# SwiGLU of a two-layer decoder trunk: three products of 256 columns per k tile in place of one of 512 and one of 256

## The chip, the cores and the metric

The kernel runs on one core of one Trainium2 chip. The metric is the device time of one execution in microseconds (us). Engines are named as the profile names them: PE is TensorE (PEld its weight loads), DVE is VectorE, ACT is ScalarE, POOL is GpSimd, SP is the engine that issues the transfers.

## The reference

Two layers over 256 tokens of width 1024, all float32. Each layer normalises x, projects it (6 parts of attention and recurrence, two gates), runs two token mixers, merges them through two projections, and adds the result to x. Then comes the part that is changed, a SwiGLU with 2816 hidden columns:

```python
h = rms_norm(x, norm_ffn[l])
x = x + (jax.nn.silu(h @ w_gate[l]) * (h @ w_up[l])) @ w_down[l]
```

## The kernel before

Everything is held transposed: 128 features on the partitions, 256 tokens (`T`) along the row. `xT` holds x in `KD` = 8 tiles of 128 features; the hidden width is `KF` = 22 such tiles.

**Products in float32 from two halves.** TensorE runs on a rounded float32 (`F32R`). So that nothing is lost, each operand a is split into a rounded part ah and the rest al, and a·b becomes ah·bh + ah·bl + al·bh. For the data, `split` (L207 to L214) does it: ScalarE writes the rounded part, VectorE the rest. For the weights, `load` (L102 to L123) fetches a chunk of about 1 MB by one transfer on SP's queue into `stage` (3 buffers), and for each half of the chunk (1024 columns, eight weight tiles) ScalarE casts it to `wh` (L118) and VectorE subtracts to get `wl` (L120). `wh` and `wl` have five buffers each. `weights` asks for a chunk and for the next one (L125 to L128).

**Two forms of the sum.** `mm3` (L216 to L229) makes the three products one by one, each of 256 columns into one result of 256 columns: L227 (ah·bh), L228 (ah·bl), L229 (al·bh). The input projections, the merge projections (L825) and the output projection (L842) use it. `mmw` (L231 to L236) is used by the SwiGLU alone. There the data tile holds bh and bl side by side (512 columns), and

```python
PE.matmul(ps, ah, b, start=i == 0, stop=False)
PE.matmul(ps[:, 0], al, b[:, 0], start=False, stop=i == n - 1)
```

makes ah·[bh bl] in one product of 512 columns (L235), then al·bh in one of 256 (L236). The result is a whole PSUM bank whose two halves have still to be added. Every product loads its own weight tile first (a LDWEIGHTS with the line of its product).

**The SwiGLU** (L849 to L886). `norm_in` (L283 to L290) splits xT times the norm's gain into `xx` and works out 1/rms per token on the way: sums of squares (L244, L246, L250), token sums on TensorE (L257, four products), a power on GpSimd (L201), and a product with ones (L275) that spreads the result over the partitions, copied to `rb` (L280). The products of the SwiGLU begin ahead of that; rb scales their results.
- Gate and up: for each m of 22, two results (j = 0 gate, j = 1 up), each over 8 k tiles. For each j: `mmw` into a bank of its own, ScalarE copies the second half out (L862), VectorE adds the first half (L863), and VectorE (j = 0) or GpSimd (j = 1) multiplies by rb (L864). Then tanh (L866), the silu (L867), the product with up on GpSimd (L869), and a split into `ff2` (L870).
- Down: for each m of 8, `mmw` over 22 k tiles into a bank, and VectorE adds both halves to xT, one after the other (L883). In the last layer each m is sent out (L885).

Eight PSUM banks are shared by four pools of two: `acc`, `prj`, `trp`, `hgp`. Even m use acc and trp, odd m hgp and prj.

**What sets the order.** Each engine works through its own queue in order. The order of the instructions in the queues is made by the scheduler of the tile framework from a simulated timeline; only the opening of layer 0 has an order written by hand (L322). Several products without their last tiles of xx can thus be begun ahead of the norm.

Of the kernel before, what the change touches and what calls it, by code (L numbers as in the profile page):

```python
# [9 lines left out]
F32 = mybir.dt.float32  # L10
# [5 lines left out]
ALU = mybir.AluOpType  # L16
AX = mybir.AxisListType

P = 128
T = 256  # L20
TT = T // P
D = 1024
KD = D // P
# [59 lines left out]
def trunk(ctx: ExitStack, tc: tile.TileContext, x_in, w_in, vec_in, gqk_in, cst_in, msk_in, out):  # L83
    nc = tc.nc
    V, S, G, PE = nc.vector, nc.scalar, nc.gpsimd, nc.tensor
# [6 lines left out]
    acc = ctx.enter_context(tc.tile_pool(name="acc", bufs=2, space=bass.MemoryType.PSUM))  # L92
    prj = ctx.enter_context(tc.tile_pool(name="prj", bufs=2, space=bass.MemoryType.PSUM))
    trp = ctx.enter_context(tc.tile_pool(name="trp", bufs=2, space=bass.MemoryType.PSUM))
    hgp = ctx.enter_context(tc.tile_pool(name="hgp", bufs=2, space=bass.MemoryType.PSUM))
# [29 lines left out]
    def weights(l, n, between=None):  # L125
        i = order.index((l, n, dict(PLAN)[n]))
        load(i + 2, between)
        return ready.pop((l, n))  # L128
# [10 lines left out]
    xT = cp.tile([P, KD, T], F32, name="xT")  # L139
# [63 lines left out]
    def bc(ap, shape):  # L203
        return ap.broadcast_to(shape)


    def split(hi, lo, src, scale=None):  # L207

        if scale is None:
            S.copy(hi, src)  # L210
            V.tensor_tensor(lo, src, hi.bitcast(F32), ALU.subtract)
        else:
            S.activation(hi, src, AF.Copy if isinstance(scale, float) else AF.Identity, scale=scale)  # L213
            V.scalar_tensor_tensor(lo, src, scale, hi.bitcast(F32), ALU.mult, ALU.subtract)  # L214

    def mm3(ps, pairs, late=False, opens=True, closes=True):  # L216
        n = len(pairs)
        if late:
            for i, ((ah, al), (bh, bl)) in enumerate(pairs):
                PE.matmul(ps, ah, bh, start=i == 0, stop=False)  # L220
                PE.matmul(ps, ah, bl, start=False, stop=False)
            for i, ((ah, al), (bh, bl)) in enumerate(pairs):
                PE.matmul(ps, al, bh, start=False, stop=i == n - 1)
            return
        shared = not (opens and closes)
        for i, ((ah, al), (bh, bl)) in enumerate(pairs):
            PE.matmul(ps, ah, bh, start=opens and i == 0, stop=False, skip_group_check=shared)  # L227
            PE.matmul(ps, ah, bl, start=False, stop=False, skip_group_check=shared)  # L228
            PE.matmul(ps, al, bh, start=False, stop=closes and i == n - 1, skip_group_check=shared)  # L229

    def mmw(ps, items):  # L231

        n = len(items)
        for i, ((ah, al), b) in enumerate(items):
            PE.matmul(ps, ah, b, start=i == 0, stop=False)  # L235
            PE.matmul(ps[:, 0], al, b[:, 0], start=False, stop=i == n - 1)  # L236

    def squares(src, kt, both=False):

# [20 lines left out]
    def token_stats(src, kt, both=False):  # L260
        return token_sums(squares(src, kt, both))

    def norm_rows(ss, meanwhile=None):

        ms = wk.tile([P, TT], F32, name="ms")
        V.tensor_scalar(ms, ss, 1.0 / D, EPS, ALU.mult, ALU.add)
        r = lay.tile([P, TT], F32, name="r")
        ins = power(r, ms)
        dg = wk.tile([P, TT, P], F32, tag="gs", name="dg")
        for t in range(TT):  # L270
            V.tensor_scalar(dg[:, t], ident, r[:, t:t + 1], None, ALU.mult)
        if meanwhile:
            meanwhile()
        ps = prj.tile([P, 512], F32, name="prj")
        PE.matmul(ps[:, :T], ones, dg.rearrange("p t c -> p (t c)"), start=True, stop=True)  # L275
        return r, ins, ps

    def norm_cols(ps):
        rb = lay.tile([P, T], F32, name="rb")
        S.copy(rb, ps[:, :T])  # L280
        return rb

    def norm_in(l, col):  # L283

        xx = lay.tile([P, KD, 2, T], F32R, name="xx")
        xh, xl = xx[:, :, 0], xx[:, :, 1]
        for k in range(KD):
            split(xh[:, k], xl[:, k], xT[:, k], vec[:, l, col + k:col + k + 1])
        r, _, ps = norm_rows(token_stats(xT, KD, both=True))
        return xx, xh, xl, r, norm_cols(ps)  # L290
# [25 lines left out]
    for l in range(L):  # L316
        opening = ExitStack()
        if l:
            xx, xh, xl, r, rb = norm_in(l, V_MIX)
        else:  # L320

            opening.enter_context(tc.manual_schedule())  # L322
            xx, ps0 = first()
            xh, xl = xx[:, :, 0], xx[:, :, 1]
# [33 lines left out]
            rb = norm_cols(said[2])  # L358
# [4 lines left out]
        xs = [(xh[:, k], xl[:, k]) for k in range(KD)]  # L363
# [173 lines left out]
        W = weights(l, "ukv")  # L537
# [4 lines left out]
        for i in range(2):  # L542
            W = weights(l, f"uq{i}")
# [18 lines left out]
        ah = mixp.tile([P, 4, T], F32R, tag="B", name="ah")  # L562
        al = mixp.tile([P, 4, T], F32R, tag="C", name="al")
# [255 lines left out]
        for i in range(2):  # L819
            Ws = [weights(l, f"proj{2 * i + c}") for c in range(2)]  # L820
            pss = [(acc.tile([P, 2, T], F32, name="acc") if c < 2 else prj.tile([P, 2, T], F32, name="prj")) for c in range(4)]
            for s, (sh, sl) in enumerate(((ah, al), (bh, bl))):
                for c in range(4):
                    o = (c % 2 * 2 + s) * 4 * P
                    mm3(pss[c][:, s], [(Ws[c // 2](o + k * P, P), (sh[:, k], sl[:, k])) for k in range(4)])  # L825
            for c in range(4):
                m = 4 * i + c
                g = wk.tile([P, 2, T], F32, name="gs", bufs=2)
# [5 lines left out]
        for i in range(4):  # L834
            W = weights(l, f"out{i}")
            ps = acc.tile([P, 2, T], F32, name="acc")

            step = KD if i else KD // 2
            for k0 in range(0, KD, step):
                for j in range(2):  # L840
                    o = j * KD * P
# [5 lines left out]


        xx, xh, xl, r, rb = norm_in(l, V_FFN)  # L849
        ffp = tc.alloc_tile_pool(name=f"ffn{l}", bufs=1)  # L850
        ff2 = ffp.tile([P, KF, 2, T], F32R, name="ff2")
        for m in range(KF):
            W = weights(l, f"gu{m}")
            if m % 2 == 0:
                pss = [acc.tile([P, 2, T], F32, name="acc"), trp.tile([P, 2, T], F32, name="trp")]
            else:
                pss = [hgp.tile([P, 2, T], F32, name="hgp"), prj.tile([P, 2, T], F32, name="prj")]
            g = ffp.tile([P, 2, T], F32, name="g", bufs=2)
            for j, ps in enumerate(pss):
                o = j * KD * P  # L860
                mmw(ps, [(W(o + k * P, P), xx[:, k]) for k in range(KD)])
                S.copy(g[:, j], ps[:, 1])  # L862
                V.tensor_tensor(g[:, j], g[:, j], ps[:, 0], ALU.add)  # L863
                (V, G)[j].tensor_tensor(g[:, j], g[:, j], rb, ALU.mult)  # L864
            th = ffp.tile([P, T], F32, name="th", bufs=2)
            S.activation(th, g[:, 0], AF.Tanh, scale=0.5)  # L866
            V.scalar_tensor_tensor(th, th, 1.0, g[:, 0], ALU.add, ALU.mult)  # L867
            hd = ffp.tile([P, T], F32, name="hd", bufs=2)
            G.tensor_tensor(hd, th, g[:, 1], ALU.mult)  # L869
            split(ff2[:, m, 0], ff2[:, m, 1], hd, 0.5)  # L870

        cur = None
        for m in range(KD):
            ps = acc.tile([P, 2, T], F32, name="acc")
            items = []
            for k in range(KF):
                i = m * KF + k
                if cur is None or cur[0] != i // 16:
                    cur = (i // 16, weights(l, f"dn{i // 16}"))
                items.append((cur[1]((i % 16) * P, P), ff2[:, k]))  # L880
            mmw(ps, items)
            for j in range(2):
                V.tensor_tensor(xT[:, m], xT[:, m], ps[:, j], ALU.add)  # L883
            if l == L - 1:
                nc.sync.dma_start(out[:, m], xT[:, m])  # L885
        ffp.release()  # L886
# [84 lines left out]
```

## Time and profile before

| | |
|---|---|
| time, median of 3 runs | 767.38 us (767.37 to 767.92) |
| profiled execution, its own time | 767.33 us |
| its span, first to last instruction | 765.5 us |
| PE busy | 758.3 us (99%), 5676 products |
| PEld busy | 693.4 us (91%), 5676 loads |
| DVE busy | 584.9 us (76%) |
| ACT busy | 443.7 us (58%) |
| POOL busy | 259.5 us (34%) |
| granted TensorE clock, mean | 0.999 |
| read from HBM | 131.11 MB, 173 GB/s over the span |

PE is a product, PEld a weight load, which overlaps products. Products are pipelined: the profile models their ends, and several are in flight at a time, so a busy PE only says that there is always one under way. How fast they follow each other is seen in the starts, in the timeline. A line such as `acc<-xx,wh` says that the tile acc is written from xx and wh; buffer numbers are left out.

### The profile page before, as it was taken

The numbers are of one execution on the slowest core, as the hardware profiler recorded it, in microseconds if no ns is written. First come the engines' busy times: TensorE is split into PE (matmuls) and PEld (weight loads), VectorE is DVE, ScalarE is ACT, GpSimd is POOL, SyncE is SP. The second block draws the span as 40 slices with busy tenths as digits, with TensorE's granted clock in tenths as the row PEclk, the third lists the DMA queues.
The fourth block names the chain that finished last, engine by engine and source line by source line (L and its number), as shares of the span: only waits on it lengthen the run. The fifth ranks groups of instructions, "written<-read, shape, count | busy, mean of one in ns | idle before, by whom it ended". The sixth has DMA issues, their size and how long they took to land.

```text
span 765.5 us, 14316 instructions
## 1 busy us (share of the span) xinstructions
PE 758.3 (99%) x5676; PEld 693.4 (91%) x5676; DVE 584.9 (76%) x866; ACT 443.7 (58%) x811; POOL 259.5 (34%) x275
## 2 busy tenths in 40 slices
PE   9999999999999999999999999999999999999998
PEld 6899999999988888888899999999998888888886
DVE  6799876678898888866667988757888988887542
ACT  6668766545465556554447796654565655655330
POOL 0685422024333443411126823201432444443000
PEclk9999999999999999999999999999999999999999
DMA  7654434436565555555534544444465555646630
GB/s 280 221 175 166 166 116 161 166 116 212 168 220 176 209 170 202 180 185 199 196 118 166 181 154 167 134 143 165 167 221 168 188 195 174 211 166 200 206 124 21
DMA packets 20802, 133.07 MB, mean 174 GB/s; under 512 B 2432, under 2 KB 3712, under 8 KB 5504
## 3 DMA queue, kind: packets, MB, share of 16 engines
q1 hardware_dynamic: 20736, 132.17, 51.0%
q8 instruction: 44, 0.72, 0.4%
q14 instruction: 22, 0.18, 0.1%
HBM read 131.11 MB, written 1.05 MB: 173 GB/s over the span
## 4 chain that ended last, share of the span: by engine, by line
PE 93%; issue 2%; POOL 1%; DVE 1%; DMA 1%; ACT 1%; SPq 1%; POOLq 0%
PE acc L235 16%; PE acc L227 11%; PE acc L229 11%; PE acc L228 10%; PE acc L236 8%; PE hgp L235 5%; PE prj L235 5%; PE trp L235 5%; PE prj L236 3%; PE trp L236 3%; PE hgp L236 3%; PE prj L227 2%; PE prj L229 2%; PE prj L228 2%; PE prj L570 1%
## 5 line engine op out<-in xcount | busy, mean ns | idle before, releaser
L120 DVE TENSOR_TENSOR wl<-st,wh 128x1024 fp32r<-128x1024 f32 (+3 forms) x241 | 322.0, 1337 | 74.1 <-ACT wh L118 72.8
L118 ACT CAST wh<-st 128x1024 fp32r<-128x1024 f32 (+3 forms) x249 | 257.1, 1038 | 139.2 <-PE acc L235 64.3
L227 PE MATMUL acc<-xx,wh 128*128 128x256 f32 x472 | 133.5, 283 | 0.0
L229 PE MATMUL acc<-xx,wl 128*128 128x256 f32 x472 | 132.3, 281 | 0.3 <-DVE wl L120 0.3
L228 PE MATMUL acc<-xx,wh 128*128 128x256 f32 x472 | 132.2, 280 | 0.0
L235 PE MATMUL acc<-ff,wh 128*128 128x512 f32 x352 | 124.3, 397 | 0.0
L236 PE MATMUL acc<-ff,wl 128*128 128x256 f32 x352 | 98.6, 281 | 0.0
L229 PEld LDWEIGHTS acc<-xx,wl 128*128 128x128 f32 x472 | 88.9, 189 | 1.4 <-issue 0.9
L227 PEld LDWEIGHTS acc<-xx,wh 128*128 128x128 f32 x472 | 89.0, 188 | 0.8 <-issue 0.2
L228 PEld LDWEIGHTS acc<-xx,wh 128*128 128x128 f32 x472 | 88.9, 188 | 0.7 <-issue 0.7
L864 POOL TENSOR_TENSOR g<-g,rb 128x256 f32<-128x256 f32 x44 | 37.2, 846 | 135.5 <-DVE g L863 123.1
L235 PEld LDWEIGHTS acc<-ff,wh 128*128 128x128 f32 x352 | 66.0, 188 | 16.2
L869 POOL TENSOR_TENSOR hd<-th,g 128x256 f32<-128x256 f32 x44 | 66.1, 1504 | 7.4 <-DVE th L867 4.5
L213 ACT ACTIVATE ff<-hd 128x256 fp32r<-128x256 f32 x44 | 18.4, 419 | 84.6 <-POOL hd L869 84.6
L236 PEld LDWEIGHTS acc<-ff,wl 128*128 128x128 f32 x352 | 66.1, 188 | 0.2
L235 PE MATMUL prj<-xx,wh 128*128 128x512 f32 x176 | 63.5, 399 | 0.0
L235 PE MATMUL acc<-xx,wh 128*128 128x512 f32 x176 | 63.3, 397 | 0.0
L235 PE MATMUL hgp<-xx,wh 128*128 128x512 f32 x176 | 63.2, 397 | 0.0
L235 PE MATMUL trp<-xx,wh 128*128 128x512 f32 x176 | 63.1, 397 | 0.0
L250 POOL TENSOR_TENSOR sq<-sq 128x256 f32<-128x256 f32 x27 | 26.3, 974 | 88.5 <-ACT sq L244 53.9
L236 PE MATMUL acc<-xx,wl 128*128 128x256 f32 x176 | 49.6, 282 | 0.0
L236 PE MATMUL hgp<-xx,wl 128*128 128x256 f32 x176 | 49.5, 281 | 0.0
(259 smaller groups left out, 1732.1 us busy)
## 6 DMA issues: line engine op xcount, KB each, us to landing
st<-in_w_dram SPq DMA_DIRECT2D x115, 1024.0 KB, 4.8
st<-in_w_dram SPq DMA_DIRECT2D x4, 1088.0 KB, 5.0
st<-in_w_dram SPq DMA_DIRECT2D x4, 576.0 KB, 3.8
st<-in_w_dram SPq DMA_DIRECT2D x3, 512.0 KB, 6.8
xT<-in_x_dram SPq DMA_DIRECT2D x4, 256.0 KB, 5.5
out_dram<-xT SPq DMA_DIRECT2D x8, 128.0 KB, 1.9
st<-in_w_dram SPq DMA_DIRECT2D x2, 256.0 KB, 4.1
cst<-in_cst_dram SPq DMA_DIRECT2D x1, 260.0 KB, 7.6
```

What stands on the lines that cost most here:

```text
L118: S.copy(wh[:, :n_], st[:, c:c + n_])
L120: eng.tensor_tensor(wl[:, :n_], st[:, c:c + n_], wh[:, :n_].bitcast(F32), ALU.subtract)
L213: S.activation(hi, src, AF.Copy if isinstance(scale, float) else AF.Identity, scale=scale)
L227: PE.matmul(ps, ah, bh, start=opens and i == 0, stop=False, skip_group_check=shared)
L228: PE.matmul(ps, ah, bl, start=False, stop=False, skip_group_check=shared)
L229: PE.matmul(ps, al, bh, start=False, stop=closes and i == n - 1, skip_group_check=shared)
L235: PE.matmul(ps, ah, b, start=i == 0, stop=False)
L236: PE.matmul(ps[:, 0], al, b[:, 0], start=False, stop=i == n - 1)
L250: G.tensor_tensor(tot, tot, sq, ALU.add)
L570: PE.matmul(pv[:, h], qT[:, h0 + h, t * P:(t + 1) * P], kT[:, h0 + h, :ns], start=True, stop=True)
L864: (V, G)[j].tensor_tensor(g[:, j], g[:, j], rb, ALU.mult)
L869: G.tensor_tensor(hd, th, g[:, 1], ALU.mult)
```

## The change

Gate and up, and down, go through `mm3` as the other projections do; `mmw` goes. The gate and the up result of one m share one bank (256 columns each), from `acc` for even and `prj` for odd m, and are scaled by rb straight from the bank by one instruction of VectorE. The copy on ScalarE, the addition on VectorE, and the scaling on GpSimd go. In down, one addition to xT takes the place of two. Weight chunks, their conversions, transfers and buffers stay.

```diff
-    def mmw(ps, items):
-
-        n = len(items)
-        for i, ((ah, al), b) in enumerate(items):
-            PE.matmul(ps, ah, b, start=i == 0, stop=False)
-            PE.matmul(ps[:, 0], al, b[:, 0], start=False, stop=i == n - 1)
...
         xx, xh, xl, r, rb = norm_in(l, V_FFN)
+        xs = [(xh[:, k], xl[:, k]) for k in range(KD)]
         ffp = tc.alloc_tile_pool(name=f"ffn{l}", bufs=1)
         ff2 = ffp.tile([P, KF, 2, T], F32R, name="ff2")
         for m in range(KF):
             W = weights(l, f"gu{m}")
-            if m % 2 == 0:
-                pss = [acc.tile([P, 2, T], F32, name="acc"), trp.tile([P, 2, T], F32, name="trp")]
-            else:
-                pss = [hgp.tile([P, 2, T], F32, name="hgp"), prj.tile([P, 2, T], F32, name="prj")]
+            ps = (acc, prj)[m % 2].tile([P, 2, T], F32, name=("acc", "prj")[m % 2])
+            for j in range(2):
+                o = j * KD * P
+                mm3(ps[:, j], [(W(o + k * P, P), xs[k]) for k in range(KD)])
             g = ffp.tile([P, 2, T], F32, name="g", bufs=2)
-            for j, ps in enumerate(pss):
-                o = j * KD * P
-                mmw(ps, [(W(o + k * P, P), xx[:, k]) for k in range(KD)])
-                S.copy(g[:, j], ps[:, 1])
-                V.tensor_tensor(g[:, j], g[:, j], ps[:, 0], ALU.add)
-                (V, G)[j].tensor_tensor(g[:, j], g[:, j], rb, ALU.mult)
+            V.tensor_tensor(g, ps, bc(rb.unsqueeze(1), [P, 2, T]), ALU.mult)
             th = ffp.tile([P, T], F32, name="th", bufs=2)
...
-                items.append((cur[1]((i % 16) * P, P), ff2[:, k]))
-            mmw(ps, items)
-            for j in range(2):
-                V.tensor_tensor(xT[:, m], xT[:, m], ps[:, j], ALU.add)
+                items.append((cur[1]((i % 16) * P, P), (ff2[:, k, 0], ff2[:, k, 1])))
+            mm3(ps[:, 0], items)
+            V.tensor_tensor(xT[:, m], xT[:, m], ps[:, 0], ALU.add)
```

## Rows read from the trace of the kernel before

**Rows 1.** The page: the span, and the chain that ended last by engine
```profile
span 765.5 us, 14316 instructions
...
PE 93%; issue 2%; POOL 1%; DVE 1%; DMA 1%; ACT 1%; SPq 1%; POOLq 0%
```

**Rows 2.** Busy time by engine and count, then granted clock (PEclk), in three stretches
```profile
core 0: us, PE busy (x) PEld busy (x) DVE busy (x) ACT busy (x) POOL busy (x), PEclk, DMA share, GB/s
220.00:320.00 100.00, 100.00 (x568) 86.89 (x567) 85.14 (x128) 57.92 (x109) 44.28 (x38) 1.00 0.56 188
...
160.00:200.00 40.00, 40.00 (x355) 40.00 (x354) 33.45 (x43) 22.28 (x33) 15.10 (x13) 1.00 0.55 186
443.00:448.00 5.00, 5.00 (x45) 5.00 (x44) 5.00 (x9) 4.87 (x14) 0.75 (x2) 1.00 0.24 43
```

**Rows 3.** Timeline of TensorE: first pair of layer 0's down projection, and what follows the 176 pairs
```profile
325.33 0.40 PE L235 MATMUL acc<-ff,wh 128*128 128x512 f32 x1
...
387.50 0.28 PE L227 MATMUL acc<-xx,wh 128*128 128x256 f32 x1
```

**Rows 4.** Timeline of TensorE, input projection of layer 1, a stretch without a break
```profile
442.75 0.28 PE L227 MATMUL acc<-xx,wh 128*128 128x256 f32 x1
...
447.81 0.28 PE L228 MATMUL acc<-xx,wh 128*128 128x256 f32 x1
```

**Rows 5.** Timeline of TensorE: first product of L842 in layer 0, and what follows the 192
```profile
178.33 0.28 PE L227 MATMUL acc<-yh,wh 128*128 128x256 f32 x1
...
200.12 0.39 PE L235 MATMUL acc<-xx,wh 128*128 128x512 f32 x1
```

**Rows 6.** Timeline of TensorE, a later input projection of layer 1, without a break
```profile
517.54 0.28 PE L227 MATMUL acc<-xx,wh 128*128 128x256 f32 x1
...
522.99 0.28 PE L227 MATMUL acc<-xx,wh 128*128 128x256 f32 x1
```

**Rows 7.** Timeline of TensorE around the ones product of layer 1's first norm
```profile
398.44 0.59 PE L275 MATMUL prj<-dg,cst 128*128 128x256 f32 x2
...
398.99 0.28 PE L227 MATMUL hgp<-xx,wh 128*128 128x256 f32 x1
399.11 0.28 PE L228 MATMUL hgp<-xx,wh 128*128 128x256 f32 x1
...
399.90 0.28 PE L229 MATMUL hgp<-xx,wl 128*128 128x256 f32 x1
```

**Rows 8.** Timeline of TensorE around the token sums of that norm
```profile
393.51 0.50 PE L257 MATMUL trp<-cst,sq 128*128 128x1 f32 x4
...
394.08 0.28 PE L229 MATMUL acc<-xx,wl 128*128 128x256 f32 x1
...
394.55 0.28 PE L227 MATMUL acc<-xx,wh 128*128 128x256 f32 x1
```

**Rows 9.** Timeline of TensorE just after the token sums ahead of layer 0's SwiGLU
```profile
207.26 0.39 PE L235 MATMUL acc<-xx,wh 128*128 128x512 f32 x1
...
207.60 0.39 PE L235 MATMUL trp<-xx,wh 128*128 128x512 f32 x1
...
207.95 0.40 PE L235 MATMUL trp<-xx,wh 128*128 128x512 f32 x1
```

**Rows 10.** The groups by line: a 512-element product with rb, DVE's addition, ACT's copy
```profile
L395 DVE TENSOR_TENSOR gs<-acc,rb 128x512 f32<-128x512 f32 x16 | 11.0, 686 | 2.7 <-PE acc L229 2.7
...
L863 DVE TENSOR_TENSOR g<-g,trp 128x256 f32<-128x256 f32 x22 | 9.1, 414 | 0.0
...
L862 ACT COPY g<-trp 128x256 f32<-128x256 f32 x22 | 8.0, 364 | 0.0
```

**Rows 11.** Timeline of DVE and ACT where layer 0's SwiGLU opens
```profile
209.92 0.41 DVE L863 TENSOR_TENSOR g<-g,acc 128x256 f32<-128x256 f32 x1
...
213.88 0.38 ACT L280 COPY rb<-prj 128x256 f32<-128x256 f32 x1
```

**Rows 12.** Timeline of the end of the run
```profile
761.91 0.87 DVE L883 TENSOR_TENSOR xT<-xT,acc 128x256 f32<-128x256 f32 x2 [6.90 <-PE acc L236]
```

## The prediction

> **What bounds the kernel now.** I read the page first: the chain of waits that ended last is TensorE for 93% of a span of 765.5 us [rows 1]. Next come the stretches of the two SwiGLUs in the table of busy time: TensorE 100%, weight loads 87%, VectorE 85%, ScalarE 58%, GpSimd 44% [rows 2]. So the time of a SwiGLU is the number of its k tiles by the time that TensorE takes for one, and the other engines count only where they leave TensorE without data. The profile's duration of a product (397 ns for 512 columns, about 280 for 256) must not be added up: products are pipelined, and the next starts long before the last has ended. What counts is the distance from one start to the next, so the third view is TensorE's timeline.
>
> For the pair of today (512 columns, then 256) it gives one answer. The 176 pairs of a down projection take 387.50 − 325.33 = 62.17 us, **353.2 ns a k tile** [rows 3], and gate and up keep the same pace. There is no waiting in it, and the last pairs of the run, with hardly a load or a conversion beside them, go no faster.
>
> For the triple of tomorrow the same trace has plenty of examples, since the input projections and the two projections ahead of the SwiGLU are made of it already. They show two paces. In one stretch 43 starts lie in 447.81 − 442.75 = 5.06 us, 117.7 ns a product, **353.0 ns a triple** [rows 4]. In another, 192 products take 200.12 − 178.33 = 21.79 us, 113.5 ns each, **340.5 ns a triple** [rows 5]; with the moving tile that the SwiGLU has, xx, it is 48 starts in 5.45 us, 113.5 too [rows 6]. I call them the long and the short pace. The granted clock is 1.00, the 2.4 GHz level, in both [rows 2], so it isn't the clock. Within an unbroken stretch the pace doesn't change for good (in the short one three products at a time fall out at a change of weight chunk, then it returns). It is drawn anew where a product of another kind comes between: after the ones product of the norm TensorE is back at the short pace after two products (399.11 to 399.90, seven starts, 113 ns) [rows 7]; after the token sums it went on at the long one (394.08 to 394.55, four starts, 117.5) [rows 8]. Of 47 such restarts in the two mixing stages I count 23 short and 24 long, in nearly the same places in both layers. The pair doesn't hold the short pace: after the token sums it has one k tile of 0.34 us, then 0.35 [rows 9], and from there 353.
>
> **The change, part by part.** The columns per k tile stay: 512 + 256 before, 3 × 256 after. So do the weight tiles, their conversion and their transfers. There are 704 k tiles in gate and up (22 × 2 × 8, two layers) and 352 in down (8 × 22, two layers), 1056 together; each gets a third weight load and a third product.
> *Pace.* Short: 340.5 − 353.2 = −12.7 ns a k tile, × 1056 = **−13.4 us**. Long: 353.0 − 353.2 = −0.2 ns, −0.2 us. I take the short pace: the stage ahead of each SwiGLU runs in it [rows 5], and the last break inside a SwiGLU is the ones product (L275), of which the one example amid triples of the same kind ended short [rows 7]; behind it some 100 us of each SwiGLU have no break, and the short pace has survived such changes of chunk. The long end stays for the range.
> The Trainium skill, "TensorE: Matmul & The Clock Gate", section "Back-to-back issue gap", speaks against this: it gives a fixed 2.5 ns for each matmul beside its columns, so a k tile with one matmul more would be slower by 2.5 ns, 2.6 us in all, about 770.0. The trace doesn't agree: three short matmuls take no longer than the pair anywhere but right behind a break.
> *The third weight load.* In stretches of triples the weight loads already fill the whole time (40.00 of 40.00 us) [rows 2], at either pace, so I price it at nothing beyond the paces; its bad bound is a rival below.
> *Getting the result out.* Per result pair, ScalarE loses two copies (364 ns), VectorE two additions (414) and a scaling (about the same), GpSimd a scaling; VectorE gains one 512-element product with rb from the bank, 686 ns by its like [rows 10]. VectorE has 3 × 414 − 686 = 556 ns less per 5.4 us. Nothing of it is on the chain, so its worth is zero; what it does is keep the weights ahead at the shorter pace: 85% of 5.65 us is 4.80, less 0.56 is 4.25, 78% of 5.45 us.
> *One bank for two results.* The bank is read once, when both are done. Eight banks before, two per m, and four after, one per m, both come round after four m (some 21 us); the evacuation, about 1 us, has that time. Price zero; were a bank late, TensorE would stop for what is missing.
> *rb is needed earlier.* Today the bank is emptied without rb; after the change the first reader needs it. In layer 0 the first result stood at 209.92, and rb's copy ended at 213.88 + 0.38 = 214.26 [rows 11]. If VectorE's queue has the scaling there, the conversions of weights behind it wait up to 4.3 us and then TensorE for them; if it is placed behind them, nothing. Bounds 0 to 4.3 us a layer; I take zero, as today's scaling by rb sits in the same queue and stands behind conversions.
> *The end.* Two additions of together 0.87 us follow the last product [rows 12]; one goes, −0.4 us. In layer 0 the same addition is covered by the products of layer 1's first projection.
> *Carried over.* The first 50 products of layer 1 follow down without a break and take its pace: 50 × 4.2 ns, −0.2 us.
> **Sum:** −13.4 − 0.4 − 0.2 = −14.0 from the profiled execution's 767.33 (span 765.5 and 1.8 around it), **753.3 us**; the median of the runs, 767.38, is the same within 0.05.
>
> **The rivals.**
> *Long pace in both SwiGLUs*: the change doesn't do what it could. For it: half the restarts went so, and a token sum too [rows 8]. Against: the ones product comes last. −0.2 − 0.4 = 766.7, no change.
> *One SwiGLU short, one long*: half of 13.4, 760.2. Against it: the restarts fall alike in both layers.
> *VectorE waits for rb* (above): decides once the wait, at most 4.3 us, exceeds the converted weights in hand, and ends slower only with the long pace: 766.7 + 2 × 4.3 = 775.3; with the short pace it leaves 761.9.
> *A third start that costs* is the other slower one: if each triple went as products do right behind a break, 0.12 us from start to start (398.99 to 399.11) [rows 7], a k tile would be 360 ns, +6.8 × 1056 = +7.2, less 0.4: 774.1. It decides where handing over to the third load isn't hidden; against it stand all long stretches of triples. The Trainium skill's fixed cost per matmul, cited above, is a weaker form of it.
>
> **How the numbers follow.** Short in both 0.53 (753.3); one of two 0.15 (760.2, and 761.9 with the wait for rb beside the short pace); long in both 0.20 (766.7); slower 0.12, of which rb 0.07 and the third start 0.05. About 0.2%, 1.5 us, is what a measurement of this kernel can tell from no change; so faster 0.68, same 0.20, slower 0.12. The range takes in all but the slower cases: from 751.5 (short pace, and some long stretches of layer 1's mixing turned short: some 400 products × 4.2 ns = 1.7 us) to 767.0 (long pace and a little of the rb wait). The likeliest case by itself spans 751.5 to 755.
>
> **What would show it.** Right: starts 113 to 114 ns apart through gate, up and down in both layers, weight loads filling the SwiGLU's stretches, each SwiGLU some 6.7 us shorter, one addition behind the last product, VectorE's share there below 80%. Wrong: 117 to 118 ns, with the time where it was; TensorE idle a few us behind the ones product, with VectorE waiting for rb; or starts 120 ns apart.

## The result, and the profile after

The changed kernel takes **757.51 us** (four executions, 757.32 to 758.40) against 767.40 before (767.37 to 767.92): ratio 0.9871, 95% interval 0.9858 to 0.9883, 9.9 us less. Ratios here leave out executions over 1.5% above a kernel's fastest; where executions are listed one by one, all are there.

The page after has the span, the busy time of the engines, and the chain that ended last:

```profile
span 755.5 us, 16139 instructions
...
PE 745.7 (99%) x6732; PEld 729.0 (96%) x6732; DVE 539.6 (71%) x762; ACT 421.8 (56%) x723; POOL 189.7 (25%) x231
...
PE 91%; DVE 4%; ACT 2%; POOL 1%; issue 1%; DMA 1%; SPq 0%; DVEq 0%; POOLq 0%; ACTq 0%
```

TensorE makes 1056 products more in less time; the chain is still its own, but VectorE now has 4% of it (1% in [rows 1]). The next view is the SwiGLU's stretches, which answer to the first of [rows 2]:

```profile
core 0: us, PE busy (x) PEld busy (x) DVE busy (x) ACT busy (x) POOL busy (x), PEclk, DMA share, GB/s
220.00:320.00 100.00, 100.00 (x885) 100.00 (x884) 71.01 (x94) 50.59 (x75) 13.86 (x19) 1.00 0.59 196
585.00:685.00 100.00, 100.00 (x885) 100.00 (x884) 71.20 (x95) 51.20 (x75) 15.06 (x20) 1.00 0.59 199
```

Some 883 starts in 100 us are 113.3 ns apart (the count takes in two or three products already under way): the short pace, in both layers. Weight loads fill the whole time, as forecast, and VectorE fell to 71%. In the timeline of TensorE the down projection of layer 0 stands between these two rows, the first its first product, the second what follows its 528:

```profile
322.60 0.28 PE L227 MATMUL acc<-ff,wh 128*128 128x256 f32 x1
...
382.44 0.28 PE L227 MATMUL acc<-xx,wh 128*128 128x256 f32 x1
```

That is 59.84 us for 176 k tiles, 340.0 ns each, where [rows 3] had 353.2. Down gained 2.33 us a layer, as much as the pace says. **Gate and up did not**: from the first product of the SwiGLU to the first of down it is 322.60 − 200.14 = 122.46 us, before 325.33 − 200.12 = 125.21 [rows 3, 5]. That is 2.75 less, where 352 k tiles at 13.2 ns make 4.65; in layer 1 it is 2.33 less (122.88 for 125.21). The timeline of TensorE at the opening shows where the rest is:

```profile
200.14 0.28 PE L227 MATMUL acc<-xx,wh 128*128 128x256 f32 x1
...
202.07 0.28 PE L229 MATMUL acc<-xx,wl 128*128 128x256 f32 x1
202.56 0.36 PE L227 MATMUL acc<-xx,wh 128*128 128x256 f32 x1 [0.22 <-DVE xT L837]
202.76 0.28 PE L228 MATMUL acc<-xx,wh 128*128 128x256 f32 x1
203.01 0.38 PE L227 MATMUL acc<-xx,wh 128*128 128x256 f32 x1
204.14 0.39 PE L229 MATMUL acc<-xx,wl 128*128 128x256 f32 x1 [0.74 <-DVE wl L120]
```

After 18 products TensorE waits twice: 202.07 to 202.56 and 203.01 to 204.14, 1.4 us more than two ordinary starts; in layer 1 the same two gaps are 0.49 and 1.48. The brackets name VectorE's addition of the output projection (L837, which gives the bank free) and a weight conversion (L120). The last view, around the ones product (now L268), answers to [rows 7]:

```profile
210.86 0.59 PE L268 MATMUL prj<-dg,cst 128*128 128x256 f32 x2
211.10 0.47 PE L227 MATMUL prj<-xx,wh 128*128 128x256 f32 x1
211.41 0.28 PE L228 MATMUL prj<-xx,wh 128*128 128x256 f32 x1
...
212.44 0.28 PE L228 MATMUL prj<-xx,wh 128*128 128x256 f32 x1
```

From 211.41 to 212.44 nine starts take 1.03 us, 114 ns each: the short pace took hold behind the ones product, as in [rows 7]. Between the token sums and the ones product the same profile has the long one (207.33 to 210.74, 29 starts, 117.6 ns).

### The profile page after: what moved, and what is told of

Its sections match the earlier page's. It is cut to its first block, busy times and chain, and to the rows that moved or that the text cites. A ratio compares the mean times of both kernels' runs of the same rounds, so it can differ in the third digit from the quotient of the medians.

```text
span 755.5 us, 16139 instructions
## 1 busy us (share of the span) xinstructions
PE 745.7 (99%) x6732; PEld 729.0 (96%) x6732; DVE 539.6 (71%) x762; ACT 421.8 (56%) x723; POOL 189.7 (25%) x231
## 4 chain that ended last, share of the span: by engine, by line
PE 91%; DVE 4%; ACT 2%; POOL 1%; issue 1%; DMA 1%; SPq 0%; DVEq 0%; POOLq 0%; ACTq 0%
PE acc L229 20%; PE acc L227 20%; PE acc L228 20%; PE prj L229 7%; PE prj L227 7%; PE prj L228 7%; DVE wl L120 2%; PE prj L563 1%; DVE xx L214 1%; PE trp L590 1%; PE trp L475 1%; ACT wh L118 1%; PE trp L584 1%; PE hgp L667 1%; DMA xT<-in_x_dram 1%
## 5 line engine op out<-in xcount | busy, mean ns | idle before, releaser
L120 DVE TENSOR_TENSOR wl<-st,wh 128x1024 fp32r<-128x1024 f32 (+3 forms) x241 | 300.7, 1249 | 133.4 <-ACT wh L118 133.1
L229 PE MATMUL acc<-xx,wl 128*128 128x256 f32 x824 | 229.6, 279 | 2.1 <-DVE wl L120 2.1
L227 PE MATMUL acc<-xx,wh 128*128 128x256 f32 x824 | 231.0, 281 | 0.4 <-DVE xT L837 0.4
L228 PE MATMUL acc<-xx,wh 128*128 128x256 f32 x824 | 229.4, 279 | 0.0
L229 PEld LDWEIGHTS acc<-xx,wl 128*128 128x128 f32 x824 | 155.0, 188 | 3.6 <-DVE wl L120 2.8
L227 PEld LDWEIGHTS acc<-xx,wh 128*128 128x128 f32 x824 | 154.9, 188 | 1.9 <-issue 0.9
L228 PEld LDWEIGHTS acc<-xx,wh 128*128 128x128 f32 x824 | 154.9, 188 | 0.7 <-issue 0.7
L227 PE MATMUL prj<-xx,wh 128*128 128x256 f32 x352 | 97.5, 277 | 0.0
L228 PE MATMUL prj<-xx,wh 128*128 128x256 f32 x352 | 97.2, 276 | 0.0
L229 PE MATMUL prj<-xx,wl 128*128 128x256 f32 x352 | 97.2, 276 | 0.0
L228 PE MATMUL acc<-ff,wh 128*128 128x256 f32 x352 | 97.1, 276 | 0.0
L227 PE MATMUL acc<-ff,wh 128*128 128x256 f32 x352 | 96.8, 276 | 0.0
L858 POOL TENSOR_TENSOR hd<-th,g 128x256 f32<-128x256 f32 x44 | 33.1, 752 | 202.8 <-DVE th L856 185.5
L227 PEld LDWEIGHTS prj<-xx,wh 128*128 128x128 f32 x352 | 66.1, 188 | 0.1
L228 PEld LDWEIGHTS prj<-xx,wh 128*128 128x128 f32 x352 | 66.1, 188 | 0.1
L229 PEld LDWEIGHTS prj<-xx,wl 128*128 128x128 f32 x352 | 66.1, 188 | 0.0
L228 PEld LDWEIGHTS acc<-ff,wh 128*128 128x128 f32 x352 | 66.1, 188 | 0.0
L227 PEld LDWEIGHTS acc<-ff,wh 128*128 128x128 f32 x352 | 65.9, 188 | 0.0
```

Source lines behind the costliest of these rows:

```text
L120: eng.tensor_tensor(wl[:, :n_], st[:, c:c + n_], wh[:, :n_].bitcast(F32), ALU.subtract)
```

## The experiments

Two questions were open: whose are the waits at the opening, and what decides the pace.

### The bank of m = 1

Run odd_hgp, the changed kernel with

```diff
-            ps = (acc, prj)[m % 2].tile([P, 2, T], F32, name=("acc", "prj")[m % 2])
+            ps = (acc, hgp)[m % 2].tile([P, 2, T], F32, name=("acc", "hgp")[m % 2])
```

> The changed kernel, with the banks of odd m taken from hgp instead of prj. Theory A (in prj the bank of m = 1 comes behind the norm's ones product, so TensorE has only m = 0 and m = 2 to begin with, and m = 2 waits for the bank of the output projection and for its converted weights): m = 1 begins before the norm, the two waits at each opening (0.38 and 1.01 us of idle time in layer 0, 0.38 and 1.36 in layer 1) go, and the time falls by about 3 us, from 757.5 to 754.4. Theory B (VectorE's conversions are late for the shorter pace, whichever bank is next): the same idle time stands elsewhere in the opening, 757.5. Both expect starts 113 to 114 ns apart behind the ones product.

> The version with the banks of odd m from hgp once more. Theory D (the pace of each SwiGLU is drawn behind the ones product): three levels again, near 754.3, 761.5 and 768.5; in the first six executions three, two and one. Theory E (always the same in one program): one level.

The order in which TensorE's products stand, by bank, changed as A said. The numbers after "acc", "hgp" are m, counts are products, "sums" and "ones" the norm's:

```
after:    acc0 18, acc2 2, acc0 1, acc2 17, acc0 3, acc2 2, sums, acc0 26, acc2 5, ones, prj1 48, ...
odd_hgp:  acc0 18, hgp1 15, acc0 1, hgp1 4, acc2 8, acc0 1, sums, acc0 28, hgp1 5, ones, hgp1 24, ...
```

The eleven executions took 768.48, 761.46, 754.09, 754.66, 762.56, 754.15 and, on another occasion, 753.86, 753.80, 769.82, 754.07, 753.96. Seven are at the level that A gave (754.4 expected), 3.4 us under the changed kernel, and in a profile at that level TensorE goes from m = 0 to m = 1 without a gap:

```profile
202.12 0.28 PE L229 MATMUL acc<-xx,wl 128*128 128x256 f32 x1
202.24 0.28 PE L227 MATMUL hgp<-xx,wh 128*128 128x256 f32 x1
```

So the waits came from the bank: B is out. The other four are at two levels some 8 and 15 us above, which D expected. The execution at 768.48 was profiled too, and its SwiGLU has the long pace (852 products in the stretch that had 885):

```profile
220.00:320.00 100.00, 100.00 (x852) 100.00 (x851) 68.38 (x90) 48.77 (x72) 13.26 (x18) 1.00 0.54 189
```

One program, the same clock, two paces: here it is the long one of [rows 4] over a whole SwiGLU. It is settled anew in each execution, but in this one not at the ones product, where D has it drawn. TensorE turned long 17 us ahead of the SwiGLU, in the output projection, amid products of one kind:

```profile
182.05 0.28 PE L227 MATMUL acc<-yh,wh 128*128 128x256 f32 x1
...
183.75 0.28 PE L227 MATMUL acc<-yh,wh 128*128 128x256 f32 x1
...
184.11 0.28 PE L227 MATMUL acc<-yh,wh 128*128 128x256 f32 x1
...
199.89 0.28 PE L227 MATMUL acc<-yh,wh 128*128 128x256 f32 x1
```

Up to 183.75 there are 15 starts at 113.3 ns, from 184.11 on 134 at 117.8; then it stayed long through the token sums (206.70 to 210.35) and the ones product. The profile of the second occasion (753.86) slips for three products at the same place and goes on short, 137 starts at 113.4:

```profile
184.33 0.28 PE L227 MATMUL acc<-yh,wh 128*128 128x256 f32 x1
...
199.86 0.28 PE L227 MATMUL acc<-yh,wh 128*128 128x256 f32 x1
```

### Which shapes can hold which pace

Run wide: `PE.matmul(ps, al, b, ...)` in place of `PE.matmul(ps[:, 0], al, b[:, 0], ...)`, so the product of the two rests is added.

> The kernel before, with the second product also made 512 columns wide (al times both halves; the result gets the small product of the two rests in addition). It asks what keeps the pair at the long pace. If it is the change of size within the pair: even sizes take the short pace, 2 x 226.7 = 453 ns a k tile, 1056 x 100 = +105 us, 873. If 512 columns hold the long pace by themselves: 2 x 235.3 = 471, +124, 891.

It took 886.93 in its one execution, between the two. A product of 512 columns takes 235 and 231 ns in turn (means over some 400 of each), neither level:

```profile
240.31 0.40 PE L235 MATMUL hgp<-xx,wh 128*128 128x512 f32 x1
240.55 0.39 PE L236 MATMUL hgp<-xx,wl 128*128 128x512 f32 x1
240.78 0.40 PE L235 MATMUL hgp<-xx,wh 128*128 128x512 f32 x1
```

Inconclusive on size against alternation; but 512 columns cost more than twice 113.5 here too.

Run down_only: the kernel before, with the down part of the change alone.

> The kernel before, with the down projections alone in the new form, gate and up as before. Theory A: 352 k tiles x 12.7 ns = 4.5 us less if the short pace takes hold, but down follows gate and up without a break, and those run in the long pace, which nothing between ends: then 353.0 a k tile, only the last addition is saved, 767.0. If the pace belongs to the shape and not to what went before: 762.6.

Ratio 0.9997, 0.9988 to 1.0006 (766.98). Down, made of triples, kept the pace it inherited from the pairs: 427 products in 50 us, 117.7 apart.

```profile
330.00:380.00 50.00, 50.00 (x427) 50.00 (x426) 29.35 (x34) 22.10 (x28) 6.23 (x6) 1.00 0.52 178
```

Run pair_ones128: the kernel before, with its ones product ahead of the SwiGLU split,

```diff
-        PE.matmul(ps[:, :T], ones, dg.rearrange("p t c -> p (t c)"), start=True, stop=True)
+        for t in range(TT):
+            PE.matmul(ps[:, t * P:(t + 1) * P], ones, dg[:, t], start=True, stop=True)
```

> The kernel before (pairs of 512 and 256 columns), with the ones product ahead of each SwiGLU made as two of 128 columns. Theory H (the pair cannot hold the short pace; the three products of 256 can): 353 ns a k tile as before in every execution, 767.3. Theory I (the pair ran long only because of what stood ahead of it): 340, where VectorE's loop of 5.59 us per m then makes TensorE wait as in the version with the split product, 766 with a granted clock of 0.993 to 0.996.

Eleven executions, 766.96 to 768.62, ratio 0.9995 (0.9987 to 1.0004). H holds: the pair starts near the short pace behind the break and loses it within five k tiles. (The kernel before does so as well behind its short output projection: the first k tile takes 0.34 us, the next 0.36, at 200.12 and 200.46.) Three k tiles from 213.32 on take 1.04 us, 347 ns each; three from 214.72 on 1.06, 353 each, and so it stays:

```profile
213.32 0.39 PE L235 MATMUL prj<-xx,wh 128*128 128x512 f32 x1
...
214.36 0.40 PE L235 MATMUL prj<-xx,wh 128*128 128x512 f32 x1
...
214.72 0.40 PE L235 MATMUL prj<-xx,wh 128*128 128x512 f32 x1
...
215.78 0.40 PE L235 MATMUL trp<-xx,wh 128*128 128x512 f32 x1
```

### The products' shape without the lighter evacuation

Run split_only, the kernel before with its `mmw` as

```diff
-            PE.matmul(ps, ah, b, start=i == 0, stop=False)
-            PE.matmul(ps[:, 0], al, b[:, 0], start=False, stop=i == n - 1)
+            PE.matmul(ps[:, 0], ah, b[:, 0], start=i == 0, stop=False, skip_group_check=True)
+            PE.matmul(ps[:, 1], ah, b[:, 1], start=False, stop=False, skip_group_check=True)
+            PE.matmul(ps[:, 0], al, b[:, 0], start=False, stop=i == n - 1, skip_group_check=True)
```

> The kernel before, with its product of 512 columns split into two of 256 into the two halves of the bank, and nothing else: banks, copies, additions and scalings as before. Theory A (the gain is the pace of TensorE and comes from the shape of the products alone): starts 113 to 114 ns apart, 1056 x 12.7 ns = 13.4 us less than before, 754.0, with four pools no idle time at the opening, VectorE's share in the SwiGLU 87% or more. Theory C (the gain comes from lighter vector engines or from the shared bank): starts 117 to 118 apart, 767 as before.

767.97, ratio 1.0003 (0.9990 to 1.0016), the profiled execution at the long pace, from its output projection on. I took that for C; it was not, as the next run shows, which has the split ones product as well.

> The kernel before with its 512-column product split into two of 256 (copies, additions and scalings as before), and the ones product ahead of each SwiGLU made as two of 128 columns. With the ones product whole, this kernel stayed at the long pace, 768. Theory F, and the results' places in the bank don't matter: short pace, 768 - 13.4 = 754.6, so that the products' shape alone is worth the whole gain. Theory G (three products that go to the two halves of a bank in turn cannot hold the short pace): 768 as before.

766.03 (ratio 0.9984, 0.9976 to 0.9992): the time is near G's, but the profile is F's. Gate and up ran at the short pace:

```profile
220.00:320.00 100.00, 100.00 (x885) 100.00 (x884) 83.80 (x127) 55.26 (x105) 44.14 (x36) 1.00 0.56 189
331.70:335.00 3.30, 3.30 (x15) 3.30 (x16) 2.72 (x6) 2.01 (x3) 0.00 (x0) 0.50 0.75 293
```

So three products that go to two halves of a bank can hold it, and the gain was lost elsewhere: at the head of down TensorE stood, and the clock granted afterwards was the lower level, 0.50, 1.2 GHz. All twelve executions have a mean granted clock of 0.993 to 0.996, which suggests that all were short and stood there; so do five of the ten of split_only, at 0.990 to 0.993. The timelines of TensorE, then of GpSimd, ScalarE and VectorE ahead of it, say why:

```profile
331.64 0.80 PE L235 MATMUL acc<-ff,wh 128*128 128x256 f32 x2 [3.62 <-ACT ff L213]
```

```profile
317.46 0.85 POOL L869 TENSOR_TENSOR g<-g,rb 128x256 f32<-128x256 f32 x1 [3.06 <-DVE g L868]
318.39 1.60 POOL L874 TENSOR_TENSOR hd<-th,g 128x256 f32<-128x256 f32 x1
323.05 0.85 POOL L869 TENSOR_TENSOR g<-g,rb 128x256 f32<-128x256 f32 x1 [3.06 <-DVE g L868]
323.98 1.60 POOL L874 TENSOR_TENSOR hd<-th,g 128x256 f32<-128x256 f32 x1
328.64 0.84 POOL L869 TENSOR_TENSOR g<-g,rb 128x256 f32<-128x256 f32 x1 [3.06 <-DVE g L868]
```

```profile
320.02 0.42 ACT L213 ACTIVATE ff<-hd 128x256 fp32r<-128x256 f32 x1 [2.44 <-POOL hd L874]
320.47 0.43 DVE L214 SCALAR_TENSOR_TENSOR ff<-hd,ff 128x256 fp32r<-128x256 f32 x1 [0.75 <-ACT ff L213]
322.55 0.41 DVE L868 TENSOR_TENSOR g<-g,trp 128x256 f32<-128x256 f32 x1
```

GpSimd scales and multiplies (L869, L874), ScalarE rounds the product (L213), VectorE takes the rest (L214), and behind that in VectorE's queue stands the addition (L868) for which GpSimd's next scaling waits. One m goes round VectorE, GpSimd, ScalarE and VectorE in 323.05 − 317.46 = 5.59 us. TensorE at the long pace needs 16 × 353.2 ns = 5.65 and never notices; at the short one 5.44, and the results fall behind by 0.15 us an m until down asks for the last. None of the three engines is full: VectorE is at 84%. The run that shortens this loop moves one instruction:

```diff
-                (V, G)[j].tensor_tensor(g[:, j], g[:, j], rb, ALU.mult)
+                V.tensor_tensor(g[:, j], g[:, j], rb, ALU.mult)
```

> As the version with the split product and the ones product of two (766.0, with TensorE standing 3.6 us at the head of each down projection), but the up result is scaled by rb on VectorE instead of GpSimd. Theory J (the results are late there because one m goes round VectorE, GpSimd, ScalarE and VectorE in 5.59 us, where TensorE needs 5.44): the loop loses GpSimd's 0.85 us and gains 0.42 on VectorE, falls below 5.44, TensorE doesn't wait, 754 to 755. Theory K (VectorE has too much to do, 84% busy): with 0.42 more per m it is later still, 767 or more.

**754.34** (ratio 0.9828, 0.9814 to 0.9841; five executions, 753.82 to 754.59). J holds: with more work on VectorE the wait is gone, and GpSimd follows TensorE:

```profile
309.19 1.64 POOL L874 TENSOR_TENSOR hd<-th,g 128x256 f32<-128x256 f32 x1 [3.80 <-DVE g L869]
314.62 1.65 POOL L874 TENSOR_TENSOR hd<-th,g 128x256 f32<-128x256 f32 x1 [3.79 <-DVE g L869]
```

5.43 us an m. The version with four pools, copies and additions is as fast as the best one with one bank: the shape of the products is worth the whole 13 us, if the short pace takes hold and what empties the banks keeps up.

### What fixes the pace

Four runs go with one another: the changed kernel again, ones128 twice, and ones1col. ones128 is odd_hgp with the split ones product, ones1col is odd_hgp with two products of one column behind the whole ones product.

> The changed kernel once more, on the chip and in the call of the next three. Theory D (the pace of each SwiGLU is drawn at the break behind the ones product, and is long in some executions): times near 757.4 (both short), 764 (one) and 771 (both long) all occur. Theory E (this kernel's order of work fixes the short pace): all within 757 to 758.5.

> The version with the banks of odd m from hgp, in which the ones product ahead of each SwiGLU is made as two products of 128 columns in place of one of 256. Theory F (what stands directly ahead of a stretch decides its pace; in the traces so far products of 128 float32 columns of the recurrence were followed by the short pace 24 times of 24): every execution short in both SwiGLUs, 754 to 755, no spread to 761 and 768 as with the ones product of 256. Theory D (a draw whatever the break): the three levels 754, 761 and 768 again.

> The same version with the ones product made as two of 128 columns, once more. If that break favours the short pace: 754 to 755.5 in all executions, as in the first four. If the first four were luck: some at 761 or 768.

> The same version, with the ones product as before and behind it, ahead of each SwiGLU, two products of one column whose results nobody reads. Theory F (products of one column, the token sums, were followed by the long pace 12 times of 12): both SwiGLUs long in every execution, 754.2 + 13.4 + 0.3 = 768, though nothing else differs. Theory D: the three levels 754, 761 and 768.

The changed kernel: 757.57, 758.12, 758.98, 757.90, with the first four all eight short in both SwiGLUs by their times; D's levels did not come, and one is 0.5 us above E's bound. ones128: 753.98 to 755.41 and 753.66 to 754.68, all eight short (ratios 0.9833 and 0.9828; 0.9821 to 0.9846 and 0.9815 to 0.9842). ones1col: 754.82 to 755.53 five times and 762.40 once, so F's rule that one column is followed by the long pace is **wrong**. The split ones product went with the short pace in all eight executions of ones128 and in all five of split_ones128_dve, and the whole one in seven of eleven with odd_hgp. But the changed kernel has the whole one and was short in all of its eight.

These counts don't show that the ones product decides, for the traces put the turn earlier. All 14 profiles have the same program up to the SwiGLU of layer 0, and its output projection ran short in ten of them and long in four (odd_hgp, split_only, down_only, pair_ones128), from the same place on, and in layer 1 each time as in layer 0. In the ten profiles whose gate and up are made of triples, the pace behind the ones product was that of the output projection in both layers, 20 of 20. In seven of them the stretch between the token sums and the ones product was long and the one behind it short, so the pace can turn at that break; where the output projection had been long (odd_hgp, split_only), it did not. No profile has triples, a long output projection and a split ones product together: whether splitting it helps is suggested by the counts and not shown, and what turns the pace stays open. ones128 and split_ones128_dve, at 754.5 and 754.3, are the fastest versions without spread, 13 us under the kernel before and 3 under the changed one.

## Why the prediction was right or wrong

- **Sign and range.** 753.3 was forecast, 751.5 to 767.0, and 757.5 came. Faster, inside the range, between the likeliest case and the next.
- **The pace** was right in kind and size: 340.0 ns a k tile for 340.5, in both SwiGLUs, behind the ones product. That it differs from execution to execution was underrated: I gave chances to the program, where odd_hgp shows all three levels in one program. And the account of where it is settled does not stand: "within an unbroken stretch the pace doesn't change for good" fails in odd_hgp, which turned long at 183.9 us in an unbroken stretch and stayed so through two breaks. That the stage ahead runs short [rows 5] was read from one execution; in four of 14 profiles it ran long. So the short pace in all eight executions of the changed kernel was forecast for a reason that is not shown, and how much of it is luck stays open.
- **"One bank for two results … Price zero"** is the step that failed. I counted when a bank comes round, and not who opens a pool first. prj also serves the norm's ones product, and trp the token sums. In the orders above, and in that of the kernel before, no result in these pools begins until that product is through. Before, m = 1 began in hgp, which the norm doesn't use; with prj its first product stands behind the ones product, and m = 2, which then comes second, needs a bank and weights that come later. It costs 1.4 us of waits in layer 0 and 1.7 in layer 1; odd_hgp, at the short pace, puts the whole at 3.4 (757.5 to 754.1). I had read that the opening of several m ahead of the norm covers the late parts of xx, and didn't carry it through the change of banks.
- **"Nothing of it is on the chain, so its worth is zero"** (copies, additions, scalings) gave the right term for the sum and for a wrong reason. What lets the short pace count is that the way out of the banks is shorter (GpSimd's scaling is gone): without that the same pace ended at 766.0 (run split_ones128), and with that alone, copies and additions kept, at 754.3 (run split_ones128_dve). I bounded it by VectorE's share, 78% afterwards; the limit was the loop of 5.59 us, and no engine's share shows it. The share itself came out at 71%, since the weight conversions (L120) also got shorter, from 1493 to 1226 ns on average between 220 and 320 us, which the sum had left as they were.
- **rb needed earlier**: at zero, as taken; the bank of m = 0 was read when rb came, with no wait of TensorE for it in the profile.
- **The end**: the addition went as forecast; from the last product to the transfer's issue it is 0.77 us (751.79 to 752.56) for 1.22 before (761.60 to 762.82; the additions in [rows 12]), but the span's end came only 0.2 earlier, 3.7 us behind that product for 3.9, so the term of −0.4 was worth half:

```profile
751.79 0.28 PE L229 MATMUL acc<-ff,wl 128*128 128x256 f32 x1
752.11 0.42 DVE L871 TENSOR_TENSOR xT<-xT,acc 128x256 f32<-128x256 f32 x1 [7.06 <-PE acc L229]
752.56 0.33 SPq L873 DMA_DIRECT2D out_dram<-xT  x1
```

- **The rivals**: a k tile made longer by its third product (a fixed cost per matmul, or a third start that isn't hidden) did not show; 1056 more products of 256 columns went through in less time. The estimate of 770.0 took 2.5 ns a matmul from the Trainium skill, "TensorE: Matmul & The Clock Gate", section "Back-to-back issue gap". That section gives the 2.5 ns for isolated matmuls, and for streams with a weight load to each about 131 ns at 512 columns, where run wide has 235 and 231; for these float32 products the measurement decides.

## What to carry to other kernels

Measure a product by the distance between starts, in a stretch without a break, before trading shapes; equal columns were not equal time here, and three products at the short pace beat two. Read the pace from more than one execution. When TensorE gets a few per cent faster, work out the time that one tile takes round the other engines, not their shares: a loop that was 1% shorter than TensorE's step became the limit. When a result moves to another pool, look at who else opens that pool, and when.

## What the runs showed of the hardware

- Products of 256 float32 columns, each with its own weights, follow one another at 113.4 or at 117.7 ns at the same granted clock of 1.00. A stretch kept its pace over more than 1500 products (behind the ones product to the end of down); another turned from the short to the long one amid products of one kind (odd_hgp, 183.9 us). The same program takes one or the other from execution to execution.
- A pair of 512 and 256 columns settled at 353 ns in every profile that has it; two of 512 in turn take 235 and 231.
- Weight loads of triples fill all of the time at either pace (100.00 of 100.00 us with 884 loads and with 851), so their share tells nothing of which one it is.
- GpSimd's product hd took 1504 ns on average before and 752 after, for the same shape (L869 and L858), with fewer of VectorE's instructions beside it; where only GpSimd's own scaling was gone (run split_ones128_dve) it still took 1.64 us. The cause was not tested:

```profile
L858 POOL TENSOR_TENSOR hd<-th,g 128x256 f32<-128x256 f32 x44 | 33.1, 752 | 202.8 <-DVE th L856 185.5
```
